# A mixed fp32 transformer stack on one core: paired splits and one bias product in the pooling mixer, side work and score banks in latent attention, the order of the NSA steps

## The chip, the cores and the metric

The kernel runs on one core of a Trainium2 chip. The metric is the device time of one execution in microseconds (us), here the median over the runs of the kernel. TensorE (PE) does the matrix products and writes PSUM, VectorE (DVE) and ScalarE (ACT) read PSUM and do the elementwise work, GpSimd (POOL) does small elementwise work in SBUF, and SyncE (SP) issues most transfers (DMAs).

## What is computed

A sequence of 512 tokens of width 1024 passes two blocks, all in fp32. Cut to what matters here:

```
first block, twice:  x = sub(x, swiglu ffn); x = sub(x, mixer); x = sub(x, swiglu ffn)
   mixer 0 = pool:   pooled[g] = centred mean over a window of 2, 4, 8, 16 tokens, group g of 256 channels
                     y = ((pooled - h)[g] @ w[g] + b[g]) * scale
   mixer 1 = mla:    lat = h @ w_in;  c_q, c_kv, k_r = split(lat), c_q and c_kv normed
                     q = c_q @ w_uq;  q_lat = q_nope @ w_uk
                     o = softmax(q_lat @ c_kv + q_rope @ k_rope) @ c_kv;  y = (o @ w_uv) @ w_o
   sub(x, f) = x + weight * (1 + gate) * norm(f(norm(x) * (1 + scale) + shift))
second block, twice: proj = norm(x) @ w_in
   y_a = stick_breaking_attention(q, k, v) * silu(z)
   y_b = (gate_c * compressed + gate_s * selected + gate_w * window attention) * silu(n_z)     (NSA)
   x = x + (sigmoid(gate_a) * (y_a @ w_up_a) + sigmoid(gate_b) * (y_b @ w_up_b)) @ w_out
```

The compressed keys and values come from blocks of 32 tokens by a small network with one hidden layer (weights `cmp_w1`, `cmp_w2`).

## The kernel before, in words

**Arithmetic.** Every fp32 operand is held as a high and a low part in a reduced format: ACT copies the high part (`split`, L244), DVE or GpSimd subtracts it from the source to get the low part (L245). A product is then three matmuls, high by high, low by high and high by low (`mm3`, L256 to L258), or two where one side is exact (`mm2`). The tiles are named `wh`, `wl` (weights), `hh`, `hl` (the normed activations), `dh`, `dl` (pooled ones), `qh`, `ql` and so on. Raw weights (`wraw`) are loaded by SP, and `split_more` (L199) splits up to three halves of 128x1024 ahead of their use.

**Order.** Each of the eight stages (ffn, pool, ffn, ffn, mla, ffn, hyb, hyb) is a list of `Item`s that `drive` (L217) runs in program order: first the weights' splits, then the item's function, then as many steps of the stage's side generator as the item's `side` gives credit for. All engines run their own instructions in the order in which this program issues them. In pool and mla the side generator (`spread`, L407) brings the three rows `rowc`, `rowb`, `rowa` of the next ffn: a DMA of each, a DMA of norm gains for two of them from ACT's queue, and a DVE product (L414) of those two.

**Pool.** The pooled difference is a banded product: per group g (0 to 3) and half z of the tokens, `band` (L702) multiplies `hh` and `hl` by constant band matrices into one bank of a two-bank PSUM tile; groups 0 and 1 share a tile, 2 and 3 another. There are four rounds over the groups: z = 0 with token tiles 0 and 1, z = 0 with tile 2, z = 1 with tiles 2 and 1, z = 1 with tile 3. At the end of the second and fourth round each group's 128x512 result is split into `dh` and `dl`. `scale` (L757) multiplies the pool weights by the output scale on DVE, `bias` (L765) splits the 1x1024 bias row, and `mix` (L772) does, per tile t and half, 12 matmuls of the pool weights and two one-row products that add the bias (L785).

**Ends of stages.** `FIN` gives, for each pair of stages, the order in which the end of one (a, b: the two product halves of a token tile; P, Z, X: norm and update of the residual `x`) is interleaved with the beginning of the next (S, A, F: norm and modulation; T: transpose; H, L: the split; G: A on GpSimd).

**Latent attention.** `lat` (L859) computes the latent of token tile t in bank `t % 2` of PSUM tile `t // 2`; `latent` norms it on DVE. `first` (L959) prepares the first four heads, then 32 units run through `attend` (L802): each iteration runs one step of several units in the order of a string. All side steps run behind `first`, whose `side` is 99.

**NSA.** In each hyb layer a preparation is written as the string `PREP`: groups of one-letter jobs, one group per item. Of its letters, a to d are the four jobs of the compression's first layer (each with two weight halves of 128x1024), w and W the window branch's projection (weights 840, 840 and 560 wide), s and q projections, p starts the norm-and-rope chain on DVE and GpSimd (reduce L1150, power L278, products L1155 to L1161), v advances it, 0 and 1 the second query projection. Capital letters A to L are fillers: gate projections of 24 matmuls of 512 columns into `gx`. `ONPOOL` names the jobs whose second half has its low part computed by GpSimd. Then 32 units (heads and branches) run through `attend` in the order of `NSO`: S scores, M row maximum, E exponential, N normalisation, T transposes, H and L their split, P the product with the values, O the fold of its result (L271), 0 and 1 further jobs: the rest of `PREP` behind the bar at 0, six matmuls of a filler at 1, from the iterations in `GAS`.

## Time and profile before

| | |
|---|---|
| median of 3 runs | 2956.75 us (2955.04 to 2959.26) |
| the profiled execution, its own time | 2962.01 us |
| its span in the trace | 2959.9 us |
| PE busy | 2806.0 us, 95% of the span |
| DVE, ACT, POOL busy | 55%, 40%, 13% |
| mean granted clock of PE | 0.962 of full speed |
| first pool products to the next ffn | about 418 to 510 us of the span |
| mla | about 1240 to 1475 us |
| NSA preparation and loop | about 2020 to 2260 us, and again 2565 to 2800 us |

A row of the timeline gives start, duration, engine, line, operation, output <- input, shape; in brackets the idle time of the engine ahead of it and what released it. PE's granted clock is 1.00 (2.4 GHz) or 0.50 (1.2 GHz); a mean between them is a mixture in time.

### The profile page before, as it was taken

The page shows a single profiled execution, that of the slowest core. Times are in us where ns is not written, and L with a number is a line of the kernel's source. Part 1 is how long each engine was busy: PE and PEld are TensorE (multiplying, and loading weights), DVE is VectorE, ACT ScalarE, POOL GpSimd, SP SyncE. Part 2 cuts the span into 40 slices and gives each one's busy share as a digit, 9 for nine tenths or more (in the row PEclk, how much of TensorE's full clock was granted, in tenths as well). Part 3 has the DMA queues.
Part 4 walks back from the last instruction along what each step waited for, and adds up shares of the span by engine and source line. Part 5 has one row for each costly group of instructions (what it writes and reads, how often), then busy time and mean ns, then how long its engine had stood idle before and what let it go on. Part 6 is the DMA issues. An engine that isn't in the chain of part 4 may idle for free.

```text
span 2959.9 us, 35318 instructions
## 1 busy us (share of the span) xinstructions
PE 2806.0 (95%) x13927; PEld 2366.0 (80%) x13927; DVE 1619.6 (55%) x2180; ACT 1169.4 (40%) x1940; POOL 376.3 (13%) x441
## 2 busy tenths in 40 slices
PE   7999988999999999979999999998899999989999
PEld 6877877888888778778788888878787887878887
DVE  5555355443355553558763233587675346767643
ACT  4223233222232223348632222384555336645531
POOL 0000012000010000147310000202131001213300
PEclk8999987999999999989999999999899999998999
DMA  7566323543336663210233333323201341231032
GB/s 242 192 202 225 107 73 107 177 169 103 107 97 198 203 204 109 60 54 30 69 117 114 100 114 95 90 62 88 63 29 58 100 142 60 76 102 37 29 100 99
DMA packets 238972, 325.74 MB, mean 110 GB/s; under 512 B 11228, under 2 KB 200896, under 8 KB 238807
## 3 DMA queue, kind: packets, MB, share of 16 engines
q1 hardware_dynamic: 237210, 317.70, 33.6%
q10 hardware_dynamic: 1596, 5.79, 0.6%
q8 instruction: 110, 1.80, 0.3%
q14 instruction: 56, 0.45, 0.0%
HBM read 317.14 MB, written 6.32 MB: 109 GB/s over the span
## 4 chain that ended last, share of the span: by engine, by line
PE 80%; DVE 8%; ACT 4%; DMA 3%; issue 2%; POOL 2%; POOLq 0%; SPq 0%; DVEq 0%; ACTq 0%
PE ps L256 21%; PE ps L257 20%; PE ps L258 20%; DMA adaw<-in_ada_w_dram 3%; PE gx L256 2%; PE gx L257 2%; PE gx L258 2%; PE pt L1248 2%; PE ps L1229 2%; DVE wl L245 1%; PE po L264 1%; PE po L263 1%; DVE wl L1027 1%; PE s L1229 1%; PE pt L1674 1%
## 5 line engine op out<-in xcount | busy, mean ns | idle before, releaser
L245 DVE TENSOR_TENSOR wl<-wraw,wh 128x1024 fp32r<-128x1024 f32 (+2 forms) x416 | 502.7, 1223 | 528.6 <-ACT wh L244 528.0
L244 ACT ACTIVATE wh<-wraw 128x1024 fp32r<-128x1024 f32 (+4 forms) x430 | 435.5, 1041 | 559.7 <-PE ps L258 308.9
L256 PE MATMUL ps<-hh,wh 128*128 128x512 f32 (+1 forms) x1648 | 639.1, 388 | 7.1 <-DVE ob L271 2.8
L257 PE MATMUL ps<-hl,wh 128*128 128x512 f32 (+1 forms) x1648 | 637.8, 387 | 2.8 <-DVE hl L468 2.8
L258 PE MATMUL ps<-hh,wl 128*128 128x512 f32 (+1 forms) x1648 | 637.2, 387 | 0.9 <-DVE wl L245 0.9
L256 PEld LDWEIGHTS ps<-hh,wh 128*128 128x128 f32 x1648 | 314.9, 191 | 71.3 <-DVE ob L271 4.2
L257 PEld LDWEIGHTS ps<-hl,wh 128*128 128x128 f32 x1648 | 314.6, 191 | 65.1 <-DVE hl L468 3.8
L258 PEld LDWEIGHTS ps<-hh,wl 128*128 128x128 f32 x1648 | 314.7, 191 | 63.2 <-DVE wl L245 1.5
L256 PE MATMUL ps<-wh,xh 128*128 128x512 f32 x800 | 313.2, 391 | 0.0
L257 PE MATMUL ps<-wl,xh 128*128 128x512 f32 x800 | 312.5, 391 | 0.0
L258 PE MATMUL ps<-wh,xl 128*128 128x512 f32 x800 | 312.3, 390 | 0.0
L361 DVE SCALAR_TENSOR_TENSOR acc<-adaw,sc,acc 128x1024 f32<-128x1024 f32 x128 | 164.1, 1282 | 151.5 <-DMA adaw<-in_ada_w_dram 151.0
L648 ACT ACTIVATE hid<-ps 128x1024 f32<-128x1024 f32 x44 | 45.1, 1028 | 400.8 <-PE ps L258 390.6
L258 PEld LDWEIGHTS ps<-wh,xl 128*128 128x128 f32 x800 | 150.6, 188 | 31.9
L256 PEld LDWEIGHTS ps<-wh,xh 128*128 128x128 f32 x800 | 150.6, 188 | 31.8
L257 PEld LDWEIGHTS ps<-wl,xh 128*128 128x128 f32 x800 | 150.6, 188 | 31.8
L277 POOL TENSOR_SCALAR s<-s 128x1 f32<-128x1 f32 x64 | 23.7, 371 | 1187.0 <-ACT junk L419 1186.1
L651 DVE TENSOR_TENSOR hid<-ps,hid 128x1024 f32<-128x1024 f32 x44 | 53.8, 1223 | 148.8 <-PE ps L258 138.9
L256 PE MATMUL gx<-hh,wh 128*128 128x512 f32 x304 | 124.3, 409 | 6.2 <-ACT scr L324 4.1
L257 PE MATMUL gx<-hl,wh 128*128 128x512 f32 x304 | 120.9, 398 | 0.0
L258 PE MATMUL gx<-hh,wl 128*128 128x512 f32 x304 | 120.9, 398 | 0.0
L256 PE MATMUL ps<-wh,hh 128*128 128x256 f32 (+3 forms) x352 | 112.8, 320 | 4.6 <-DVE scr L847 3.0
(496 smaller groups left out, 4841.5 us busy)
## 6 DMA issues: line engine op xcount, KB each, us to landing
wraw<-in_ffn_w_in_dram SPq DMA_DIRECT2D x86, 1024.0 KB
adaw<-in_ada_w_dram SPq DMA_DIRECT2D x128, 512.0 KB
wraw<-in_ffn_w_out_dram SPq DMA_DIRECT2D x88, 512.0 KB
wraw<-in_w_in_dram SPq DMA_DIRECT2D x52, 512.0 KB
wraw<-in_w_in_dram SPq DMA_DIRECT2D x14, 1024.0 KB
adaw<-in_ada_w_dram SPq DMA_DIRECT2D x32, 256.0 KB
wraw<-in_cmp_w_dram SPq DMA_DIRECT2D x16, 512.0 KB
wraw<-in_w_out_dram SPq DMA_DIRECT2D x16, 512.0 KB
```

Of the source, the lines that this page charges most:

```text
L244: self.nc.scalar.activation(h, src, AF.Copy)
L245: (eng or self.nc.vector).tensor_tensor(l, src, h.bitcast(F32), op=OP.subtract)
L256: mm(out, w[0], x[0], start=start, stop=False)
L257: mm(out, w[0], x[1], start=False, stop=False)
L258: mm(out, w[1], x[0], start=False, stop=stop)
L263: mm(out, v, xh, start=start, stop=False)
L264: mm(out, v, xl, start=False, stop=stop)
L361: nc.vector.scalar_tensor_tensor(acc, raws[q][:, k], self.sc[:, f:f + 1], acc, op0=OP.mult, op1=OP.add)
L648: nc.scalar.activation(st["hid", it], ps, AF.Silu)
L651: nc.vector.tensor_tensor(h, ps, h, op=OP.mult)
L1229: mm(sc[:, f], q[:, c], k[:, 0:n], start=m == 0 and (g == 1 or i == 0), stop=False)
L1248: nc.tensor.transpose(t[:, k], d["p"][:, f.start + k * 128:f.start + k * 128 + 128], self.ident)
```

## The change

In pool, two groups are split at once (128x1024), in the second and fourth rounds after groups 1 and 3. The bias is one tile of 128 rows, zero but for its high part in row 0 and its low part in row 32, and one product with 128 rows adds both. The scaling of weights, the bias split and the side steps stand at other items, A of tile 1 is on DVE instead of GpSimd at pool's entry, and at its exit Z of tile 1 stands behind F of tile 0. In mla the latent of tile t is in PSUM tile `t % 2`, bank `t // 2`, and the side steps run at one per four iterations. In NSA, `PREP`, `ONPOOL` and `NSO` are other strings, items with p may split four halves ahead, and one filler, L, stands in the preparation, so that five instead of six remain for the loop (iterations 6 to 25; the last number of `GAS` is not reached).

```diff
-           ("ffn", "pool"): "... b1 P1 Z1 H0 L0 a2 X1 G1 S1 b2 Z2 ..."
-           ("pool", "ffn"): "... a1 b1 Z1 P1 a2 F0 T0 X1 A1 ..."
+           ("ffn", "pool"): "... b1 P1 Z1 H0 L0 a2 X1 A1 S1 b2 Z2 ..."
+           ("pool", "ffn"): "... a1 b1 P1 a2 F0 Z1 T0 X1 A1 ..."
-    NSO, NSD, NNE = "HES1LPMNO0T", (-1, -2, -3), 1
-    PREP, ONPOOL = "s x q vv p0 ab w1 vBvWc vId vvCkJztK|uvZ e v f - - - - g - h", "csa"
+    NSO, NSD, NNE = "HE1LSMN0POT", (-1, -2, -3), 1
+    PREP, ONPOOL = "s x q vv p 0ab wL1 BvvWc vId vvCkJztK|uZ e v f - - - - g - h", "ad"
-    GAS = (6, 10, 14, 18, 22, 26)
+    GAS = (6, 10, 14, 18, 22, 28)
@@ split_more
-            if n >= self.done and (n >= self.done + 3 or ...
+            if n >= self.done and (n >= self.done + self.items[self.now].ahead or ...
@@ pool
-            st["b"] = tuple(P.tile([1, D], F32R, name=n) for n in ("pbh", "pbl"))
+            st["b"] = P.tile([128, D], F32R, name="pbhl")
+            nc.gpsimd.memset(st["b"].bitcast(F32), 0.0)
-            if last_:
+            if last_ and g % 2:
-                self.split(st["dh"][:, 2 * g:2 * g + 2, ts], st["dl"][:, 2 * g:2 * g + 2, ts], ps...)
+                self.split(st["dh"][:, 2 * g - 2:2 * g + 2, ts], st["dl"][:, 2 * g - 2:2 * g + 2, ts],
+                           st["ps", z, g // 2].rearrange("p a (m n) -> p (a m) n", m=2))
-            items.append(Item(part(g, 0, (2,), False, True, g == 0), [], g == 3))
+            items.append(Item(part(g, 0, (2,), False, True, g == 0), [], g > 1))
-            items.append(Item(part(g, 1, (2, 1), True, False, 0), [], 0))
+            items.append(Item(part(g, 1, (2, 1), True, False, 0), [], g < 2))
-            items.append(Item(part(g, 1, (3,), False, True, g == 0), [], 1 if g < 3 else 99))
+            items.append(Item(part(g, 1, (3,), False, True, g == 0), [], 0 if g < 3 else 99))
-            self.split(*st["b"], st["pb"], nc.gpsimd)
-        for k, f in ((5, lambda: scale(0)), (8, lambda: scale(1)), (15, bias)):
+            self.split(st["b"][0:1], st["b"][32:33], st["pb"])
+        for k, f in ((4, lambda: scale(0)), (12, lambda: scale(1)), (14, bias)):
-                for z in st["b"]:
-                    nc.tensor.matmul(ps[:, half], self.ones[0:1, :], z[:, half * 512:half * 512 + 512], ...)
+                nc.tensor.matmul(ps[:, half], self.ones, st["b"][:, half * 512:half * 512 + 512], ...)
@@ attend, mla
-            items.append(Item(fn, w, 0, hold))
+            items.append(Item(fn, w, side, hold))
-                o = ps[t // 2][:, t % 2, 0:416]
+                o = ps[t % 2][:, t // 2, 0:416]
-        items.append(Item(first, quad_w(0), 99))
+        items.append(Item(first, quad_w(0), 1))
-        items += self.attend(32, steps, self.ORDER, slices)
+        items += self.attend(32, steps, self.ORDER, slices, 0.25)
@@ hyb
-            items.append(Item(self.group(g, jobs), weights(g), 0, hold(g)))
+            items.append(Item(self.group(g, jobs), weights(g), 0, hold(g), 4 if "p" in g else 3))
```

VectorE in the pool stage, from the split of the second round's results to the weights' splits ahead of the products. `dl` is the low part of the pooled difference, `hl` that of the activations of token tile 3, `rowc` a row of the next ffn, `pb` the bias row. Before:

```order
L245 TENSOR_TENSOR dl<-ps,dh 128x2x256 [waits Activation_49] x2
L761 TENSOR_TENSOR wraw<-wraw,srow 128x1024 [waits DMAHW6_49,DMAHW4_49]
L245 TENSOR_TENSOR dl<-ps,dh 128x2x256 [waits Activation_49] x2
L761 TENSOR_TENSOR wraw<-wraw,srow 128x1024 [waits DMAHW5_49]
L763 TENSOR_TENSOR pb<-pb,srow 1x1024 [waits DMAHW7_49]
L468 TENSOR_TENSOR hl<-scr,hh 128x1024 [waits DVE_49,Activation_49]
L245 TENSOR_TENSOR dl<-ps,dh 128x2x256 [waits Activation_49]
L414 SCALAR_TENSOR_TENSOR rowc<-rowc,adaw 128x1024 [waits DMAHW2_49,DMAHW1_49]
L245 TENSOR_TENSOR wl<-wraw,wh 128x1024 [waits DVE_49,Activation_49]
```

With the change:

```order
L763 TENSOR_TENSOR wraw<-wraw,srow 128x1024 [waits DMAHW6_49,DMAHW4_49]
L245 TENSOR_TENSOR dl<-ps,dh 128x4x256 [waits Activation_49] x2
L414 SCALAR_TENSOR_TENSOR rowc<-rowc,adaw 128x1024 [waits DMAHW2_49,DMAHW1_49]
L468 TENSOR_TENSOR hl<-scr,hh 128x1024 [waits Activation_49]
L763 TENSOR_TENSOR wraw<-wraw,srow 128x1024 [waits DMAHW5_49]
L765 TENSOR_TENSOR pb<-pb,srow 1x1024 [waits DMAHW7_49]
L245 TENSOR_TENSOR wl<-wraw,wh 128x1024 [waits Activation_49] x2
L245 TENSOR_TENSOR dl<-ps,dh 128x4x256 [waits Activation_49]
L245 TENSOR_TENSOR pbhl<-pb,pbhl 1x1024 [waits Activation_49]
L245 TENSOR_TENSOR dl<-ps,dh 128x4x256 [waits Activation_49]
```

The splits are twice as wide and half as many, the product of `rowc` has moved ahead of `hl`, and the low part of the bias has come to this engine.

VectorE in latent attention, from the last key split (`kl`) of `first` to the second unit's row maximum (`mx`). Before:

```order
L252 TENSOR_TENSOR kl_7775<-pt,kh_7774 64x512 [waits PE_49,Activation_49]
L252 TENSOR_TENSOR kl_7777<-pt,kh_7776 64x512
L414 SCALAR_TENSOR_TENSOR rowc<-rowc,adaw 128x1024 [waits DMAHW5_49,DMAHW0_49]
L414 SCALAR_TENSOR_TENSOR rowa<-rowa,adaw 128x1024 [waits DMAHW7_49,DMAHW1_49]
L991 TENSOR_REDUCE mx<-ps 128x2 [waits PE_49] x2
L1002 RECIPROCAL mx<-mx 128x2 [waits Activation_49]
L1005 TENSOR_SCALAR p<-p,mx 128x512 [waits DVE_49]
L245 TENSOR_TENSOR ql<-pt,qh 96x512 [waits Activation_49]
L991 TENSOR_REDUCE mx<-ps 128x2 [waits PE_49]
```

With the change:

```order
L252 TENSOR_TENSOR kl_7759<-pt,kh_7758 64x512 [waits PE_49,Activation_49]
L252 TENSOR_TENSOR kl_7761<-pt,kh_7760 64x512
L991 TENSOR_REDUCE mx<-ps 128x2 [waits PE_49] x2
L1002 RECIPROCAL mx<-mx 128x2 [waits Activation_49]
L1005 TENSOR_SCALAR p<-p,mx 128x512 [waits DVE_49]
L245 TENSOR_TENSOR ql<-pt,qh 96x512 [waits Activation_49]
L414 SCALAR_TENSOR_TENSOR rowc<-rowc,adaw 128x1024 [waits DMAHW6_49,DMAHW5_49]
L991 TENSOR_REDUCE mx<-ps 128x2 [waits PE_49]
```

The products of `rowc` and `rowa` stood ahead of the first maximum; now `rowc` stands behind the first two units' steps, and `rowa` (not shown) twelve units later.

VectorE in the NSA preparation of the first hyb layer. `ob` is the last row of the norm-and-rope chain that p starts, `wl` of 1024 columns here the second half of job b, `wl` of 840 and 560 columns the window's weights. Before:

```order
L1160 TENSOR_TENSOR scr<-scr,t_0_12778 128x8x32
L1161 TENSOR_TENSOR ob<-ob,scr 128x2x256 [waits DVE_49]
L245 TENSOR_TENSOR wl<-wraw,wh 128x1024 [waits DMAHW1_49,Activation_49]
L245 TENSOR_TENSOR wl<-wraw,wh 128x840 [waits DMAHW2_49,Activation_49]
L245 TENSOR_TENSOR wl<-wraw,wh 128x840 [waits DMAHW7_49,DMAHW3_49,Activation_49]
L245 TENSOR_TENSOR wl<-wraw,wh 128x560 [waits DMAHW4_49,Activation_49]
```

With the change, the chain's beginning (`nv` is a split of the s job's result, `r` the chain's reductions):

```order
L252 TENSOR_TENSOR nv_14024<-gx,nv_14024 128x2x64 [waits Activation_49]
L252 TENSOR_TENSOR nv_14024<-gx,nv_14024 128x2x64
L245 TENSOR_TENSOR wl<-wraw,wh 128x1024 [waits DMAHW0_49,Activation_49]
L245 TENSOR_TENSOR wl<-wraw,wh 128x1024 [waits DMAHW1_49,Activation_49]
L1150 TENSOR_REDUCE r_14086<-scr 128x8
```

and its end:

```order
L1160 TENSOR_TENSOR scr<-scr,t_0_12762 128x8x32
L1161 TENSOR_TENSOR ob<-ob,scr 128x2x256 [waits DVE_49]
L245 TENSOR_TENSOR wl<-wraw,wh 128x840 [waits DMAHW2_49,Activation_49]
L245 TENSOR_TENSOR wl<-wraw,wh 128x840 [waits DMAHW7_49,DMAHW3_49,Activation_49]
L245 TENSOR_TENSOR wl<-wraw,wh 128x560 [waits DMAHW7_49,Activation_49]
L245 TENSOR_TENSOR wl<-wraw,wh 128x1024 [waits DMAHW0_49,Activation_49]
```

Both halves of job b now stand ahead of the chain; the window's splits still stand behind its last row, and the split of the moved filler L (1024 columns) behind them.

## Rows read from the trace of the kernel before

**Rows 1.** The page, part 1: busy time of the engines, share of the span, instructions.

```profile
PE 2806.0 (95%) x13927; PEld 2366.0 (80%) x13927; DVE 1619.6 (55%) x2180; ACT 1169.4 (40%) x1940; POOL 376.3 (13%) x441
```

**Rows 2.** Windows: start:end, length, busy time (x instructions) of PE, PEld, DVE, ACT, POOL, PE's granted clock, DMA share, GB/s.

```profile
426.00:453.50 27.50, 19.34 (x88) 18.53 (x87) 15.70 (x18) 9.50 (x13) 2.84 (x3) 0.50 0.39 127
457.00:474.00 17.00, 17.00 (x64) 13.51 (x63) 11.48 (x10) 4.99 (x8) 2.40 (x6) 0.51 0.01 1
...
1305.00:1450.00 145.00, 136.12 (x882) 121.24 (x882) 127.92 (x217) 123.87 (x280) 104.63 (x101) 0.98 0.07 22
2187.67:2202.13 14.46, 14.46 (x96) 12.84 (x94) 10.26 (x30) 8.34 (x27) 5.65 (x5) 1.00 0.15 51
```

**Rows 3.** Timeline of PE in the pool stage: the rounds, the first products, the end.

```profile
419.94 0.33 PE L721 MATMUL ps<-wh,hl 128*128 128x136 f32 x1 [1.38 <-DVE hl L468]
...
429.98 0.38 PE L716 MATMUL ps<-wh,hh 128*128 128x8 f32 x1 [1.80 <-DVE dl L245]
...
435.01 0.56 PE L716 MATMUL ps<-wh,hh 128*128 128x256 f32 x1
...
441.84 0.46 PE L716 MATMUL ps<-wh,hh 128*128 128x136 f32 x1
...
449.38 0.48 PE L716 MATMUL ps<-wh,hh 128*128 128x136 f32 x1 [1.77 <-DVE dl L245]
...
450.73 0.52 PE L256 MATMUL ps<-wh,dh 128*128 128x256 f32 x1
...
454.98 0.49 PE L785 MATMUL ps<-pbl,ones 1*128 1x512 f32 x1 [1.02 <-POOL pbl L245]
...
457.22 0.79 PE L785 MATMUL ps<-pbh,ones 1*128 1x512 f32 x1
...
458.37 0.58 PE L256 MATMUL ps<-wh,dh 128*128 128x256 f32 x1
...
486.25 1.06 PE L451 MATMUL ps<-ident,scr 128*128 128x128 f32 x8 [2.45 <-DVE scr L442]
```

**Rows 4.** Timeline of POOL and of DVE in the pool stage.

```profile
412.39 2.41 POOL L438 TENSOR_TENSOR scr<-x,rowa 128x1024 f32<-128x1024 f32 x1 [2.94 <-DVE x L529]
...
438.70 1.21 DVE L468 TENSOR_TENSOR hl<-scr,hh 128x1024 fp32r<-128x1024 f32 x1
```

**Rows 5.** Timeline of PE in latent attention: second latent, first scores of the loop.

```profile
1271.51 0.43 PE L256 MATMUL ps<-wh,hh 128*128 128x416 f32 x1 [2.48 <-DVE scr L847]
...
1305.03 0.80 PE L256 MATMUL ps<-kh,qh 96*128 96x512 f32 x1 [6.09 <-ACT p L997]
```

**Rows 6.** Timeline of DVE in latent attention, around the loop's start.

```profile
1296.92 1.39 DVE L252 TENSOR_TENSOR kl<-pt,kh 64x512 fp32r<-64x512 f32 x2 [0.46 <-ACT kh L250]
1299.75 1.22 DVE L414 SCALAR_TENSOR_TENSOR rowc<-rowc,adaw 128x1024 f32<-128x1024 f32 x1 [1.44 <-DMA adaw<-in_norm_g_dram]
...
1302.27 2.36 DVE L991 TENSOR_REDUCE mx<-ps 128x2 f32<-128x1024 f32 x2
```

**Rows 7.** Timeline of PE, then of DVE, in the first NSA preparation.

```profile
2050.94 0.48 PE L257 MATMUL pt<-wl,qAh 128*64 128x256 f32 x1 [8.45 <-DVE wl L245]
...
2053.58 0.43 PE L257 MATMUL ps<-wl,hh 128*128 128x280 f32 x1
...
2038.48 1.91 DVE L1150 TENSOR_REDUCE r<-scr 128x8 f32<-128x512 f32 x4
...
2049.66 3.10 DVE L245 TENSOR_TENSOR wl<-wraw,wh 128x1024 fp32r<-128x1024 f32 x3
```

**Rows 8.** Timeline of PE in the first NSA loop: scores of two units, a filler.

```profile
2138.39 0.46 PE L1229 MATMUL s<-kth,qAl 128*128 128x128 f32 x1
...
2144.52 0.31 PE L1229 MATMUL s<-kth,qAl 128*128 128x128 f32 x1
...
2152.26 0.40 PE L256 MATMUL gx<-hh,wh 128*128 128x512 f32 x1
2152.49 0.39 PE L257 MATMUL gx<-hl,wh 128*128 128x512 f32 x1
```

More of the change, by code (lines that the diff above doesn't have):

```diff
@@ L101, with __init__ @@
 class Item:
-    def __init__(self, fn, w=(), side=1, hold=0):
-        self.fn, self.w, self.side, self.hold = fn, list(w), side, hold
+    def __init__(self, fn, w=(), side=1, hold=0, ahead=3):
+        self.fn, self.w, self.side, self.hold, self.ahead = fn, list(w), side, hold, ahead
 class Kern:
     FIN = {("ffn", "ffn"): "a0 b0 P0 Z0 X0 S0 A0 a1 F0 b1 P1 Z1 a2 T0 X1 H0 A1 b2 S1 L0 F1 P2 Z2 a3 T1 X2 H1 L1 w0 G2 b3 P3 S2 Z3 X3 A3 F2 S3 F3||T2 H2 T3 H3 L2 L3",
[2 rows of a table removed]
[2 rows of a table added]
            ("ffn", "mla"): "a0 b0 P0 Z0 X0 S0 A0 F0 a1 b1 a2 P1 T0 Z1 X1 A1 H0 S1 L0 b2 F1 P2 Z2 w0 X2 a3 T1 H1 S2 A2 b3 Z3 F2 P3 L1 X3 G3 T2|H2 S3 L2 F3 T3|H3 L3",
@@ L201, in split_more @@
             n = self.nsplit
-            if n >= self.done and (n >= self.done + 3 or self.halves[n].item - self.now > self.halves[n].late or (n >= SLOTS and self.halves[n - SLOTS].last > self.now - back)):
+            if n >= self.done and (n >= self.done + self.items[self.now].ahead or self.halves[n].item - self.now > self.halves[n].late or (n >= SLOTS and self.halves[n - SLOTS].last > self.now - back)):
                 break
@@ L783, in product @@
                                  g % 2 == 0 and k == 0, False)
-                for z in st["b"]:
-                    nc.tensor.matmul(ps[:, half], self.ones[0:1, :], z[:, half * 512:half * 512 + 512], start=False,
-                                     stop=z is st["b"][1])
+                nc.tensor.matmul(ps[:, half], self.ones, st["b"][:, half * 512:half * 512 + 512], start=False, stop=True)
                 return ps.rearrange("p a b -> p (a b)") if half else None
@@ L800, in parts, with attend @@
         return lanes, w, hold
-    def attend(self, n, steps, order, slices):
+    def attend(self, n, steps, order, slices, side=0):
         items = []
```

1 line of the change is left out of this document (removed), and 4 rows, old and new, of the table FIN.

## The prediction

> **What bounds the kernel now.** The page first: PE is busy 2806.0 of 2959.9 us, 95% [rows 1]. Nearly all of the program is PE's own work, so the change can win only where PE waits or runs at half clock. I therefore read PE's timeline for waits of the three stages that the diff touches, then the engine that released each wait, then windows for the clock.
>
> In **pool**, PE is busy 19.34 of 27.50 us between 426 and 453.5, at a granted clock of 0.50, that is 1.2 GHz [rows 2]. Four of its waits there are for a `dl` split of DVE: 1.80 is the first, 1.77 the last, the two between are 2.29 and 1.41, 7.3 us in all [rows 3]. They are false ones. The waiting matmul writes the second bank of a PSUM tile whose first bank is being split for the group before; nothing that it needs is missing. In the products PE is busy all the time from 457 to 474 and still has 0.51 of its clock [rows 2].
>
> In **latent attention** PE waits 2.48 us for the norm of the tile before, which sits in the other bank of its PSUM tile, and 6.09 us before the loop [rows 5]. DVE's rows show why the second is so long: the last key split ends at 1298.31, `rowc` then waits 1.44 for its gains, two products follow, and only at 1302.27 comes the maximum on which the first exponential rests [rows 6].
>
> In **NSA** the largest wait of each preparation is 8.45 us, for the low part of the second half of job b [rows 7]; the second hyb layer has the same wait. DVE does that split at 2049.66, behind the norm-and-rope chain that began at 2038.48.
>
> **Pool, part by part.** Splitting in pairs takes the four waits away: the round's next group starts in the bank beside, nobody reads that tile. Gain 7.3 us. The order shows no PE wait on DVE there any more except those for `hl` and the bands' low parts. A of tile 1 moves from GpSimd, 2.41 us [rows 4], to DVE, where the wide rows take 1.21 [rows 4]; PE's wait of 1.38 on `hl` at 419.94 [rows 3] is behind it, so 1.2. The first product then starts at 450.73 - 8.5 = 442.2 [rows 3].
>
> What could be late instead is `hl` of token tile 3, for the fourth round. It was done at 438.70 + 1.21 = 439.9 [rows 4], two us ahead of that round at 441.84 [rows 3]; now the round begins 1.2 + 1.80 + 2.29 = 5.3 us sooner, at 436.5, and on DVE two wide splits and `rowc`'s product stand ahead of `hl`. From the end of the second round, which lies one round of 441.84 - 435.01 = 6.8 us earlier [rows 3], it takes a wide copy on ACT, a wide subtraction, `rowc` and `hl`, about 1.1 + 1.2 + 1.2 + 1.2 = 4.7. That leaves two us. `rowc`'s product also waits for a DMA of gains; in latent attention that wait was 1.44 [rows 6]. So I cost it at nothing; beyond two us, each us of the DMA is one of PE.
>
> The bias: eight pairs of one-row products become eight products. A pair paces 458.37 - 457.22 = 1.15 us at half clock [rows 3]; a 512-column matmul takes 0.23 at full clock [rows 8], so about 0.46 at half. That is 0.7 each, 5.5 in all at half clock, half of that at full. The wait of 1.02 on GpSimd's low part [rows 3] goes too: DVE does it. Not all of this arrives, because the stage ends on a chain of norms and updates, shown by PE's 2.45 us wait for DVE at 486.25 [rows 3]. Bounds: nothing and 6.5; I take 4.4, since PE is busy without a pause through most of the products. Z of tile 1 behind F of tile 0 is DVE work moved within that chain; I put it into the bounds. Sum for pool: 7.3 + 1.2 + 4.4 = 12.9.
>
> **The clock in the products.** The row shows PE busy for all 17.00 us and the clock at 0.51 [rows 2]: being busy did not bring the clock back for most of them. The Trainium skill says otherwise ("TensorE: Matmul & The Clock Gate", Part 1, "What's actually happening"): the half rate is the idle state, and sustained matmul activity releases it. By that page these products, with PE never idle, should run at 2.4 GHz, and 17.00 us of work would take 8.5 less. The sum above goes by the row, with no change in clock; the other outcome is a rival below.
>
> **Latent attention.** With tile t in PSUM tile `t % 2`, the second latent writes where nothing is read: 2.48 gone. The third now waits for the norm of the first, done long before. Taking the two `rowc`/`rowa` products from ahead of the maximum lets DVE begin at 1298.3 instead of 1302.27: 4.0. They cost 1.22 each inside the loop [rows 6], where DVE is busy 127.92 and PE 136.12 of 145 us [rows 2]. Neither engine is full, so of the 2.4 I charge half. Sum: 2.5 + 4.0 - 1.2 = 5.3. Bounds: 0.1 if the loop's start is held by something else and both products cost in full; 6.5 if they cost nothing there.
>
> **NSA, each of two layers.** Both splits of b now stand ahead of the chain, so the 8.45 us wait for b goes. But the window's splits still stand behind the chain, and PE wants the window next. The chain starts one split of 1.1 us later, and a split of 1024 columns takes 3.10 / 3 = 1.0, so one of 840 about 0.9 [rows 7]: window data at about 2049.66 + 1.1 + 0.9 = 2051.7, against 2053.3 when PE began it before (its second matmul is at 2053.58 [rows 7]). So the wait is not removed but moved by one job, and 1.6 is what is gained; it would be 8.45 if the window came in time, and nothing if the added splits push the chain more.
>
> The filler L, 24 matmuls of 0.23 us [rows 8], is 5.45 us of PE work that moves from loop iterations 26 to 29 into the preparation; there it stands behind a late split and fills no wait. Without it four units of the loop can be faster than now. Now four units take 14.46 us with PE busy for all of it [rows 2], 3.61 each. The units before the fillers begin took (2144.52 - 2138.39) / 2 = 3.06 [rows 8], so 2.2 is gained for four; DVE's 10.26 us for four [rows 2] bounds the gain at 4.2. I take 3.2. The new order inside the loop (S behind the filler, O behind P) I cost at nothing, since PE has no wait there to begin with; what covers it is the slack of the other engines, and what it costs without that is the last rival. Sum per layer: 1.6 - 5.45 + 3.2 = -0.7, two layers -1.4, with bounds of +7.2 and -5.5 for each.
>
> **Sum.** 12.9 + 5.3 - 1.4 = 16.8 us. The profiled execution took 2962.01, 5.3 above the median of the runs, 2956.75; so 2945.2 for it, and 2940 as a median.
>
> **The rivals.**
>
> The clock comes back in the products. For it: the one-row products, which use one of 128 rows, and the waits ahead of the products are gone. Against: the windows' 0.51 at a full PE. Time: 2940 - 8.5 = 2931.5. Chance 0.18.
>
> The NSA wait really goes, because the window's splits come in time. For it: halves may now be split four ahead; against: the order still has them behind the chain. It would give 2 x (8.45 - 1.6) = 13.7 more: 2926. Chance 0.08.
>
> The last units of the loop do not become faster, since each waits for its own exponentials and folds, and L is paid in full: 2 x 3.2 = 6.4 less gain, 2946. Chance 0.16.
>
> The change does not free the rounds in pool: `hl` of tile 3 is late by the DMA of the gains, and the 8.5 us come back as one wait. 2948.5. Chance 0.06.
>
> Slower: S now stands behind the filler instead of ahead of it, so that in a unit with a filler the next scores, their maximum and their exponential come 6 x 0.23 = 1.4 us later [rows 8]. Where that chain through DVE and ACT has less slack than this, PE's transposes wait for it in each of the 2 x 20 units with fillers. Half of the 1.4 showing makes 40 x 0.7 = 28: 2968. The gain of the rest is used up from 0.42 a unit on. For it: the chain goes through three engines, and DVE is busy for 10.26 of the 14.46 us of four units [rows 2]. Against: PE shows no wait at all there now, and S is issued a whole unit before its transposes. Chance 0.06.
>
> **How the numbers follow.** The forecast keeps 0.46, with a range of its own of 2933 to 2947 from the bounds of bias, `rowc` and loop. The range of 8 in 10, 2923 to 2951, takes in all rivals but the slower one. A measurement of this kernel can tell 0.2%, about 6 us, from no change. Faster by more: 0.85. Within: 0.09, for cases where the third and fourth rivals meet. Slower: 0.06.
>
> **What would show it.** Right: no PE wait on `dl` between 426 and 450, the first product about 8.5 us earlier; the wait before the loop of latent attention at about 2 us; in NSA no wait for b, but one of 6 to 8 us for a window split; loop units of 3.61 us with fillers and about 2.8 without. Wrong: a wait on `hl` in the fourth round, units above 3.7 us with fillers, or a preparation longer by over 5 us.

## The result and the profile after

The changed kernel takes 2926.25 us (median of 3 runs, 2925.72 to 2930.96) against 2956.75: a ratio of 0.99 with a 95% interval of 0.9886 to 0.9913. That is 30.5 us less, where 16.8 were forecast. The time lies in the range, but below the likeliest case's own 2933 to 2947. Timed again beside the last two experiments, the same kernel took 2927.5 against 2957.54 (0.9903, 0.9888 to 0.9917).

The profiled execution took 2930.96, with a span of 2929.2, against 2962.01 and 2959.9. The page's first part, to be held against [rows 1]: PE is busy for 17.6 us less, and 13.1 of the 30.7 are time in which it stood.

```profile
PE 2788.4 (95%) x13919; PEld 2352.2 (80%) x13919; DVE 1619.1 (55%) x2180; ACT 1168.4 (40%) x1936; POOL 365.1 (12%) x438
```

Where they went is read from the stages. I cut the span at PE instructions that both kernels have: pool from its first band product to the wait of the next ffn for its weights; latent attention from its first latent to its first scores, and from there to the output projection; each NSA layer from the transposes behind the stick-breaking branch to the first window product, to the first compressed scores, and to the merge. Windows of the kernel before (columns as in [rows 2]): pool, latents, attention loop, then preparation and loop of the first NSA layer and of the second.

```profile
417.60:503.30 85.70, 66.21 (x353) 58.30 (x352) 51.03 (x50) 31.76 (x47) 22.08 (x26) 0.72 0.28 93
1247.90:1295.50 47.60, 36.19 (x162) 32.66 (x160) 20.63 (x47) 14.84 (x38) 20.22 (x37) 0.82 0.18 60
1295.50:1451.70 156.20, 139.80 (x900) 123.73 (x898) 136.40 (x226) 129.30 (x290) 104.63 (x101) 0.98 0.09 29
2053.30:2122.10 68.80, 61.90 (x367) 54.08 (x365) 41.86 (x80) 34.15 (x66) 11.92 (x14) 0.94 0.39 105
2122.10:2257.20 135.10, 126.09 (x749) 111.83 (x750) 100.94 (x264) 78.16 (x223) 45.72 (x34) 0.88 0.09 28
2597.60:2665.20 67.60, 61.15 (x366) 53.68 (x364) 41.96 (x80) 34.26 (x66) 11.94 (x14) 0.95 0.40 107
2665.20:2798.10 132.90, 123.48 (x750) 109.65 (x750) 100.93 (x264) 78.65 (x223) 45.72 (x34) 0.90 0.10 29
```

The same stages of the changed kernel:

```profile
417.60:489.80 72.20, 54.54 (x346) 51.99 (x345) 50.99 (x48) 30.95 (x42) 21.85 (x26) 0.81 0.33 110
1233.80:1275.10 41.30, 32.85 (x161) 30.17 (x160) 20.61 (x47) 14.86 (x38) 20.02 (x37) 0.88 0.15 44
1275.10:1428.10 153.00, 138.86 (x899) 122.91 (x897) 136.90 (x226) 129.71 (x290) 108.13 (x101) 0.99 0.11 36
2020.90:2100.10 79.20, 68.21 (x388) 59.77 (x388) 51.42 (x95) 35.76 (x69) 14.95 (x18) 0.91 0.35 95
2100.10:2226.70 126.60, 115.83 (x726) 101.62 (x726) 98.47 (x263) 76.43 (x221) 43.38 (x33) 0.93 0.09 26
2558.30:2638.90 80.60, 69.38 (x389) 60.45 (x389) 51.40 (x95) 36.34 (x69) 14.90 (x18) 0.89 0.35 94
2638.90:2767.40 128.50, 119.08 (x725) 105.04 (x725) 99.12 (x263) 76.02 (x221) 43.24 (x33) 0.89 0.08 26
```

Pool is 13.5 us shorter, the latents 6.3, the attention loop 3.2. The piece ahead of the window, not in these rows, falls from 34.7 to 26.3 us in both NSA layers, since its wait of 8.45 is gone and 1.20 is left; with it the preparation is 2.0 and 4.6 longer and the loop 8.5 and 4.4 shorter. So the first layer gains 6.5, and the second loses 0.3. 13.5 + 6.3 + 3.2 + 6.5 - 0.3 = 29.2 of the 30.7 in the span; the rest lies in stages that the change doesn't touch.

**Pool.** PE's timeline of the changed kernel shows no wait for `dl` any more. Ahead of the fourth round its other waits were there before too: 0.78 for the second tile's `hl` (1.38 [rows 3]), 2.09 for the bands' low parts (2.08), 1.04 for the third tile's `hl` (0.88). In the fourth round there is a new one, of 2.12, for the last tile's `hl`; the first product comes 26.6 us after the first band product instead of 33.1 [rows 3]. The bias is one product of 128 rows.

```profile
419.33 0.33 PE L722 MATMUL ps<-wh,hl 128*128 128x136 f32 x1 [0.78 <-DVE hl L468]
...
439.50 0.48 PE L722 MATMUL ps<-wh,hl 128*128 128x136 f32 x1 [2.12 <-DVE hl L468]
...
444.26 0.52 PE L256 MATMUL ps<-wh,dh 128*128 128x256 f32 x1
...
449.90 0.41 PE L786 MATMUL ps<-pbhl,ones 128*128 128x512 f32 x1
450.15 0.28 PE L256 MATMUL ps<-wh,dh 128*128 128x256 f32 x1
...
451.59 0.40 PE L786 MATMUL ps<-pbhl,ones 128*128 128x512 f32 x1
```

DVE's timeline says what that 2.12 is: after the second round's two wide splits DVE stands at `rowc`'s product for 4.64 us, for the DMA of the gains, and `hl` is behind it in the queue.

```profile
431.22 1.23 DVE L245 TENSOR_TENSOR dl<-ps,dh 128x1024 fp32r<-128x1024 f32 x1 [0.23 <-ACT dh L244]
437.08 1.23 DVE L414 SCALAR_TENSOR_TENSOR rowc<-rowc,adaw 128x1024 f32<-128x1024 f32 x1 [4.64 <-DMA adaw<-in_norm_g_dram]
438.23 1.22 DVE L468 TENSOR_TENSOR hl<-scr,hh 128x1024 fp32r<-128x1024 f32 x1
```

**Latent attention.** The 2.48 us ahead of the second latent [rows 5] are gone, and the wait at the loop's start is 2.19 instead of 6.09. DVE goes from the last key split straight to the maximum; `rowc` comes inside the loop.

```profile
1280.70 0.50 PE L256 MATMUL ps<-kh,qh 96*128 96x512 f32 x1 [2.19 <-ACT p L997]
```

```profile
1276.52 1.39 DVE L252 TENSOR_TENSOR kl<-pt,kh 64x512 fp32r<-64x512 f32 x2 [0.47 <-ACT kh L250]
1277.95 2.36 DVE L991 TENSOR_REDUCE mx<-ps 128x2 f32<-128x1024 f32 x2
```

**NSA.** The wait for b of 8.45 [rows 7] is gone; one of 6.22 for the window's low part stands in its place, and 1.20 ahead of it. L begins at 2036.45 (first NSA layer, PE).

```profile
2020.89 0.37 PE L256 MATMUL ps<-wh,hh 128*128 128x280 f32 x1 [1.20 <-DVE scr L1155]
2027.48 0.60 PE L257 MATMUL ps<-wl,hh 128*128 128x280 f32 x1 [6.22 <-DVE wl L245]
...
2036.45 0.39 PE L256 MATMUL gx<-hh,wh 128*128 128x512 f32 x1
```

In the loop, units with a filler keep their pace (2156.24 to 2199.52, 12 units, 3.61 us each, as in [rows 2]). The four that lost theirs are this window: 9.74 us, 2.44 each.

```profile
2199.52:2209.26 9.74, 9.24 (x70) 8.27 (x68) 8.36 (x27) 6.74 (x23) 4.31 (x3) 1.00 0.00 1
```

### The profile page after: what moved, and what is told of

Read it like the earlier page. It is cut to its first block, busy times and chain, and to the rows that moved or that the text cites. A ratio compares the mean times of both kernels' runs of the same rounds, so it can differ in the third digit from the quotient of the medians.

```text
span 2929.2 us, 35287 instructions
## 1 busy us (share of the span) xinstructions
PE 2788.4 (95%) x13919; PEld 2352.2 (80%) x13919; DVE 1619.1 (55%) x2180; ACT 1168.4 (40%) x1936; POOL 365.1 (12%) x438
## 4 chain that ended last, share of the span: by engine, by line
PE 78%; DVE 9%; DMA 4%; ACT 4%; issue 3%; POOL 2%; SPq 0%; DVEq 0%; POOLq 0%; ACTq 0%
PE ps L257 20%; PE ps L256 20%; PE ps L258 20%; DMA adaw<-in_ada_w_dram 3%; PE gx L256 2%; PE gx L257 2%; PE gx L258 2%; PE ps L1229 2%; PE pt L1248 2%; DVE wl L245 1%; PE po L264 1%; PE po L263 1%; DVE wl L1027 1%; DVE mx L991 1%; PE pt L1674 1%
## 5 line engine op out<-in xcount | busy, mean ns | idle before, releaser
L245 DVE TENSOR_TENSOR wl<-wraw,wh 128x1024 fp32r<-128x1024 f32 (+1 forms) x418 | 504.9, 1223 | 525.8 <-ACT wh L244 525.1
L244 ACT ACTIVATE wh<-wraw 128x1024 fp32r<-128x1024 f32 (+3 forms) x430 | 436.0, 1041 | 572.5 <-PE ps L258 308.1
L277 POOL TENSOR_SCALAR s<-s 128x1 f32<-128x1 f32 x64 | 26.3, 410 | 1200.4 <-ACT junk L419 1199.3
L256 PE MATMUL gx<-hh,wh 128*128 128x512 f32 x304 | 126.6, 417 | 6.5 <-ACT scr L324 4.1
L257 PE MATMUL ps<-wl,hh 128*128 128x256 f32 (+3 forms) x352 | 112.5, 320 | 12.4 <-DVE wl L245 12.4
```

What stands on the lines that cost most here:

```text
L244: self.nc.scalar.activation(h, src, AF.Copy)
L245: (eng or self.nc.vector).tensor_tensor(l, src, h.bitcast(F32), op=OP.subtract)
L256: mm(out, w[0], x[0], start=start, stop=False)
L257: mm(out, w[0], x[1], start=False, stop=False)
```

## Experiments

Stage lengths in us as defined above, each from one profiled execution; "prep" is both pieces of an NSA preparation together.

| kernel | median (runs) | pool, to first product / rest | latents / loop | NSA 1, prep / loop | NSA 2, prep / loop |
|---|---|---|---|---|---|
| before | 2956.75 (3) | 33.1 / 52.6 | 47.6 / 156.2 | 103.5 / 135.1 | 102.3 / 132.8 |
| changed | 2926.25 (3) | 26.6 / 45.5 | 41.3 / 153.1 | 105.5 / 126.6 | 106.9 / 128.5 |
| pool alone | 2940.24 (4) | 26.8 / 46.8 | 46.4 / 155.7 | 103.3 / 135.0 | 102.3 / 132.9 |
| pairs alone | 2947.68 (1) | 25.0 / 53.0 | 43.8 / 156.5 | 103.3 / 135.1 | 102.3 / 132.9 |
| bias alone | 2953.02 (1) | 33.1 / 49.2 | 46.6 / 155.7 | 104.7 / 133.2 | 102.4 / 132.9 |
| latent attention alone | 2948.88 (9) | 33.1 / 49.7 | 40.1 / 152.8 | 103.4 / 135.1 | 102.3 / 132.9 |
| side steps alone | 2958.16 (1) | 33.1 / 52.5 | 44.7 / 154.4 | 103.6 / 135.1 | 102.4 / 132.9 |
| NSA alone | 2946.12 (5) | 33.1 / 52.5 | 44.4 / 156.0 | 105.6 / 128.3 | 106.3 / 128.4 |
| changed, old loop order | 2928.34 (1) | 27.7 / 45.3 | 41.3 / 153.5 | 105.9 / 126.4 | 106.9 / 127.6 |
| changed, L in the loop | 2944.86 (1) | 26.3 / 45.4 | 40.1 / 152.4 | 105.7 / 133.2 | 107.3 / 133.2 |
| changed, old prep with L | 2924.40 (1) | 26.9 / 45.3 | 39.9 / 153.0 | 107.0 / 127.4 | 109.6 / 127.4 |
| changed, `hl` first | 2928.08 (4) | 24.3 / 45.4 | 40.1 / 152.3 | 105.8 / 127.3 | 106.8 / 128.5 |

Kernels that were timed together share their runs of the kernel before: 2955.95 for the four with several runs here, 2954.07 and 2954.13 for those with one. A single time says little (the last 7 runs of the kernel before spread from 2950.39 to 2959.9); of those kernels the stages are read.

**The three parts alone.** First pool's lines of the diff in the kernel before, then those of latent attention, then those of NSA; the cores of them are:

```diff
-            if last_:
+            if last_ and g % 2:
...
+                nc.tensor.matmul(ps[:, half], self.ones, st["b"][:, half * 512:half * 512 + 512], start=False, stop=True)
```

> The kernel before with the pool part of the change alone (paired splits, one bias product, the items of scaling, bias and side steps, both FIN strings); latent attention and NSA are the old code. Theory 1 (the sum by stages): the pool stage, from its first band product to the next ffn's wait for its weights, is 13.5 us shorter, as in the changed kernel, so about 2943 us. Of the two NSA stages, whose code is untouched, theory 1a says that their length depends on where the granted clock happens to fall in them, so that one of them (238.6 and 235.1 us before, from the last transposes of the stick-breaking part to the merge's first product) differs by over 2 us from before; theory 1b says that a stage with the same code keeps its length within 1 us, and that what the changed kernel won in the first NSA stage (6.5 us) and not in the second (0.3 us lost) comes from its own edit.

```diff
-                o = ps[t // 2][:, t % 2, 0:416]
+                o = ps[t % 2][:, t // 2, 0:416]
...
-        items.append(Item(first, quad_w(0), 99))
+        items.append(Item(first, quad_w(0), 1))
```

> The kernel before with the latent attention part alone (PSUM banks of the latent, side steps spread over the loop). Theory 1: 9.4 us shorter in that stage, as in the changed kernel, so about 2947 us: 2.5 from the latent's wait, 4 from the loop's start, 3 from the half clock that no longer follows the 6 us wait. Rival: the loop pays for the two row products, the stage gains the forecast 5.3 and the rest of the changed kernel's gain there comes from the pool part's shift in time; then about 2951. The untouched NSA stages test the clock as in the run of the pool part: over 2 us different in one of them by theory 1a, within 1 us by 1b.

```diff
-    PREP, ONPOOL = "s x q vv p0 ab w1 vBvWc vId vvCkJztK|uvZ e v f - - - - g - h", "csa"
+    PREP, ONPOOL = "s x q vv p 0ab wL1 BvvWc vId vvCkJztK|uZ e v f - - - - g - h", "ad"
```

> The kernel before with the NSA part alone (PREP, ONPOOL, NSO, four halves ahead). Theory 1a (the edit gives back in the preparation what it wins in the loop, and the clock decides the rest): between 2953 and 2960, and the two NSA stages change by different amounts. Rival 1b (the edit itself is worth about 6 us in the first layer): the first stage is 6.5 us shorter again and the second 0.3 us longer, about 2950.5. In both the wait of 8.45 us for job b is gone and one of about 6.2 us for the window's low part stands in its place.

Measured: 0.9947 (0.993 to 0.9964), 0.9978 (0.9967 to 0.9988) and 0.9965 (0.9952 to 0.9978) of the kernel before, which is 15.7, 7.1 and 9.8 us less. Together 32.6; the whole change had 30.5. The parts add up within their uncertainty. By the medians each of them gains more than its term of the forecast; the intervals, about 11 to 21, 4 to 10 and 7 to 14 us, leave that open for pool (12.9 forecast) and latent attention (5.3), and not for NSA (-1.4). By its stages the NSA part alone gains 5.0.

The second NSA layer, where a kernel leaves it alone, keeps its length however far the program ahead of it has moved: it is within 102.3 to 102.4 and 132.8 to 132.9 in all six kernels with the old NSA lines. Other stages don't. The stretch ahead of the pool stage took 409.3 to 417.6 us in the 14 profiled executions, though the edits reach no more than its last items; in the stretch from 20 to 40 us the granted clock was 0.66 in the kernel before and 0.80 in the changed kernel with the old preparation and L, which are the two ends. So a single time can differ by 8 us without the edit. The latents vary too: with the old lines between 43.8 and 47.6, with the new ones between 39.9 and 41.3. So some of the 6.3 us of the profiled pair is scatter, and the kernel with latent attention alone, timed in nine runs, gives the better size, 7.1 (3.5 to 9.8) for that whole part.

**Pairs alone and bias alone.** Pool's gain, taken apart.

```diff
-            if last_:
+            if last_ and g % 2:
```

> The kernel before with the paired splits of pool alone: the two one-row bias products, the items of scaling and side steps and both FIN strings stay old. Theory (two separate gains): the four waits for dl go, the first product comes about 7 us after fewer than before (33.1 us after the first band product before, about 26 here), and the rest of the stage keeps its 52.6 us with some 11 us lost to the half clock, since the one-row products are still there. Rival (the waits are what keeps the clock low): the rest shrinks as well, by 5 us or more, with less half clock in it, as in the run of the whole pool part (46.8).

```diff
-                for z in st["b"]:
-                    nc.tensor.matmul(ps[:, half], self.ones[0:1, :], z[:, half * 512:half * 512 + 512], start=False,
-                                     stop=z is st["b"][1])
+                nc.tensor.matmul(ps[:, half], self.ones, st["b"][:, half * 512:half * 512 + 512], start=False, stop=True)
```

> The kernel before with the one bias product of 128 rows (and its low part on VectorE) alone. Theory: the first product stays at 33.1 us, the rest of the pool stage shrinks from 52.6 to about 47, because the clock is back at its full level for most of the products: eight one-row pairs, during which one of 128 rows works, are gone. Rival: the clock stays, and only the shorter products count: the rest shrinks by 2 to 4 us.

Each part does its own half of the stage: the pairs bring the first product 8.1 us sooner (33.1 to 25.0) and leave the rest at 53.0; the bias leaves the first and shortens the rest by 3.4. What the bias does besides its own instructions shows in windows of 17 us in the products, to be held against 457 to 474 of the kernel before, with PE busy all the time at 0.51 [rows 2]. With the pairs of splits alone, one-row products kept:

```profile
446.00:463.00 17.00, 17.00 (x64) 13.50 (x63) 11.08 (x10) 4.59 (x8) 2.85 (x6) 0.50 0.03 13
```

With the 128-row product alone:

```profile
451.50:468.50 17.00, 11.41 (x76) 10.70 (x75) 14.45 (x13) 5.72 (x12) 3.92 (x10) 0.80 0.01 2
```

And in the changed kernel:

```profile
450.50:467.50 17.00, 12.05 (x95) 11.01 (x93) 14.55 (x12) 8.38 (x13) 6.67 (x11) 1.00 0.01 1
```

The stretch with a 128-row product runs at 2.4 GHz, that with one-row products mostly at 1.2. It is not a clean switch. Of the 96 products of 256 columns, counted in PE's timeline, those that took 0.40 us or less (0.41 and more is half clock) were 40 to 42 in four of the kernels with one-row products (before, pairs, NSA, side steps alone), 63 in the fifth (latent attention alone), and 71 to 78 in the nine executions with the 128-row product. In the kernel with 63 the clock came up between one-row products; it fell again 1.2 us behind a wait of 1.68 and then stayed low with PE busy:

```profile
446.00:463.00 17.00, 14.46 (x82) 11.69 (x83) 9.02 (x8) 5.86 (x9) 5.34 (x7) 0.89 0.37 132
463.00:470.00 7.00, 7.00 (x30) 5.90 (x29) 6.69 (x6) 3.29 (x5) 1.48 (x4) 0.53 0.01 2
```

```profile
462.19 1.06 PE L451 MATMUL ps<-ident,scr 128*128 128x128 f32 x8 [1.68 <-DVE scr L442]
```

In the changed kernel PE waits 2.51 and 1.72 us at the same step, and the products behind those waits stay at full clock. Two things differ between the two kinds of bias product, the rows (1 or 128) and the number (two or one), and no run takes them apart.

With bias alone the last bias product comes 24.4 us after the first product instead of 29.4, with PE busy for 18.6 of them instead of 28.4, and yet the stage's rest is only 3.4 shorter: among the products PE now waits for DVE's step of the norm.

```profile
460.94 1.94 PE L451 MATMUL ps<-ident,scr 128*128 128x128 f32 x8 [5.46 <-DVE scr L442]
```

DVE is late there because the product of `rowa` has stood 4.01 us for the DMA of its row, with the norm's steps behind it in the queue:

```profile
452.31 1.23 DVE L414 SCALAR_TENSOR_TENSOR rowa<-rowa,adaw 128x1024 f32<-128x1024 f32 x1 [4.01 <-DMA rowa<-vec]
```

In the changed kernel, whose side steps stand at other items, that product comes at 447.53 without a wait, and the first wait of PE of that kind is 2.51. With the whole pool part the rest is 45.3 to 46.8, shorter than with the bias alone. The side steps, the scaling of the weights and the two FIN strings were not run by themselves, so what each of them has of this is not shown.

**`hl` first.** The changed kernel with `rowc`'s product behind `hl`, by the side credits of the second and fourth rounds.

```diff
-            items.append(Item(part(g, 0, (2,), False, True, g == 0), [], g > 1))
+            items.append(Item(part(g, 0, (2,), False, True, g == 0), [], g == 2))
...
-            items.append(Item(part(g, 1, (2, 1), True, False, 0), [], g < 2))
+            items.append(Item(part(g, 1, (2, 1), True, False, 0), [], 0))
...
-            items.append(Item(part(g, 1, (3,), False, True, g == 0), [], 0 if g < 3 else 99))
+            items.append(Item(part(g, 1, (3,), False, True, g == 0), [], (3, 0, 0, 99)[g]))
```

> The changed kernel with the product of rowc on VectorE moved behind hl of token tile 3 (side steps at other items of pool). In the changed kernel that product waits 4.64 us for the DMA of the gains, hl stands behind it, and PE waits 2.12 us for hl in the fourth round. Theory: that wait goes, the first product of pool comes 2.1 us sooner, about 2924 us. Rival: the products wait for the weights' low parts instead, which now stand behind the late rowc; then the first product moves by less than 1 us and the time stays at 2926. A shift of the clock's spells may add or take some us to either in later stages.

`hl` is now done before the fourth round wants it, the gains are waited for behind it, and the first product comes 24.3 us after the first band product, 2.3 sooner:

```profile
431.83 1.22 DVE L468 TENSOR_TENSOR hl<-scr,hh 128x1024 fp32r<-128x1024 f32 x1
...
436.43 1.23 DVE L414 SCALAR_TENSOR_TENSOR rowc<-rowc,adaw 128x1024 f32<-128x1024 f32 x1 [1.13 <-DMA adaw<-in_norm_g_dram]
```

So the wait of 2.12 was the gains' DMA, one wait in the place of others. The median of 2928.08 (0.9903, 0.9888 to 0.9919) is not below that of the changed kernel, so both were timed once more, in turn, in five rounds.

> The changed kernel itself once more, beside the next one, so that the two are timed in turn on one chip: 2924 to 2931 as it was.

> The changed kernel with the gains' product behind hl in pooling, once more. Its pool stage was 2.5 us shorter (the wait of 2.12 for hl is gone) in one profiled execution each, while the medians did not differ. Theory: the 2.5 us are real and last, so this one is 1.5 to 3 below the other of the same call. Rival: the chain that ends the pool stage, or what half clock the stages behind it have, takes them back: within 1 us of each other.

Pool took 71.4 and 69.7 us, the medians were 2927.5 (2926.93 to 2930.0) and 2924.15 (2918.75 to 2927.71), the ratios 0.9903 (0.9888 to 0.9917) and 0.9884 (0.9865 to 0.9902). The stage is shorter by about two us each time; for the kernel the intervals overlap, and the two pairs of medians disagree in sign. It beats the kernel before; that it beats the changed one is not shown.

**Side steps alone.** The two credits of latent attention, with the latents' banks as before.

```diff
-        items.append(Item(first, quad_w(0), 99))
+        items.append(Item(first, quad_w(0), 1))
...
-        items += self.attend(32, steps, self.ORDER, slices)
+        items += self.attend(32, steps, self.ORDER, slices, 0.25)
```

> The kernel before with the two side credits of latent attention alone (the first loop item 99 to 1, the loop's items 0 to 0.25); the banks of the latent products stay as they were. Theory: the loop's wait for the side work goes (6.09 us at its start falls to about 2), the latent stretch falls by 3 to 4 to some 44 us, and the loop falls from 156.2 to about 153 because no stretch of it runs at half clock; the 2.48 us wait between the latent products stays. Layer 197 to 198, kernel 2949 to 2952. Rival of the forecast's own sum: the loop has two more row products and gets 1.2 us longer, layer near 201, kernel 2953 to 2954.

The 6.09 us at the loop's start became 2.22, and the 2.49 between the latents stayed:

```profile
1267.33 0.43 PE L256 MATMUL ps<-wh,hh 128*128 128x416 f32 x1 [2.49 <-DVE scr L847]
...
1297.07 0.50 PE L256 MATMUL ps<-kh,qh 96*128 96x512 f32 x1 [2.22 <-ACT p L997]
```

The loop is 1.8 us shorter where 3.9 of wait went, at the same granted clock of 0.98, so 2.1 of other waits came in; I put them down to the two products. With the banks as well (latent attention alone) it is 3.4 shorter. That the kernel's single time is not lower is within the spread of single times.

**The loop's order.** The changed kernel with the old string of steps.

```diff
-    NSO, NSD, NNE = "HE1LSMN0POT", (-1, -2, -3), 1
+    NSO, NSD, NNE = "HES1LPMNO0T", (-1, -2, -3), 1
```

> The changed kernel with the old order string of the NSA loop (S ahead of the filler, the fold behind M and N). Theory: the loop's gain over before (8.5 us in the first layer, 4.3 in the second) comes from the missing filler (2 to 4 us of each) and from less half clock, and the order string is worth under 1.5 us per layer: loops of 126 to 128 us and 128 to 130. Rival: the order string is what lets the loop start and end sooner; then the loops are 3 us or more longer than 126.6 and 128.5.

Loops of 126.4 and 127.6 against 126.6 and 128.5 (and 128.2 and 128.6 in the second execution of the changed kernel). The order of the steps is worth nothing that can be told here; the forecast's slower rival, S behind the filler, has no price.

**L back in the loop.** The changed kernel, with the sixth filler in iterations 26 to 29 again.

```diff
-    PREP, ONPOOL = "s x q vv p 0ab wL1 BvvWc vId vvCkJztK|uZ e v f - - - - g - h", "ad"
+    PREP, ONPOOL = "s x q vv p 0ab w1 BvvWc vId vvCkJztK|uZ e v f - - - - g - h", "ad"
...
-    GAS = (6, 10, 14, 18, 22, 28)
+    GAS = (6, 10, 14, 18, 22, 26)
```

> The changed kernel with the filler L back in the loop (iterations 26 to 29), all else as changed. Theory: the preparation, from the window's first product to the first compressed scores, is 5.5 us or more shorter than the changed kernel's 79.2 and 80.6 us, the loop 2 to 4 us longer per layer, so that leaving L in the loop is better by 1 to 3 us per layer: about 2922. Rival: L in the preparation keeps the clock up there, and the loop without it ends sooner by as much as L costs: no difference, or the changed kernel ahead by 2 us or more per layer.

Without L the preparation is not shorter: 105.7 and 107.3 against 105.5 and 106.9. In L's place PE waits 3.34 us for the norm-and-rope products of DVE, a wait that the changed kernel does not have:

```profile
2028.18 0.60 PE L257 MATMUL ps<-wl,hh 128*128 128x280 f32 x1 [6.22 <-DVE wl L245]
...
2050.56 0.37 PE L256 MATMUL ps<-wh,hh 128*128 128x280 f32 x1 [3.34 <-DVE scr L1155]
```

In the loop L costs 6.6 and 4.7 us. So L's move is worth 6.8 and 5.1, and the other edits of the preparation, without L, lose 2.2 and 5.0 in the preparation (105.7 and 107.3 against 103.5 and 102.3).

What makes up these differences can be read from the second piece of the preparation (2021.59 to 2101.01 and 2566.23 to 2647.23 in this kernel). In the first layer PE stands there for 14.6 us without L and for 11.0 with it; the other part of L's price comes back by the clock, 0.89 without it and 0.91 with it. What the other edits lose is mostly clock as well. Against the kernel before, over both pieces, PE stands for 15.8 us instead of 15.4 in the first layer and 15.8 instead of 14.9 in the second, but it is busy 1.9 and 4.2 us longer with the same number of products. The granted clock in the second piece is 0.89 and 0.85, where it was 0.94 and 0.95.

**The old preparation with L.** The changed kernel, with the steps and the splits of the preparation as before, but L behind w.

```diff
-    PREP, ONPOOL = "s x q vv p 0ab wL1 BvvWc vId vvCkJztK|uZ e v f - - - - g - h", "ad"
+    PREP, ONPOOL = "s x q vv p0 ab wL1 vBvWc vId vvCkJztK|uvZ e v f - - - - g - h", "csa"
...
-            items.append(Item(self.group(g, jobs), weights(g), 0, hold(g), 4 if "p" in g else 3))
+            items.append(Item(self.group(g, jobs), weights(g), 0, hold(g), 3))
```

> The changed kernel, but the NSA preparation keeps the order of before (steps, splits on the vector engine or not, three items ahead) with the one step L put in behind w; so the loop has lost L as in the change. Theory: what the NSA part gains comes from L's absence in the loop alone, and the other edits of the preparation only pull a wait for b out of it and put a wait for wl in. Then the first NSA layer keeps its loop near 127 us and its stretch up to the window goes back from 26.3 to 34.7, with a preparation of 69 to 72, some 231 to 234 in all; the second layer 34.7 + 69 + 128, some 231 to 233; kernel 2922 to 2929. Rival: only in the new order is there a gap that L fills, and in the old order L costs its full 5 us on PE in the preparation: then the preparation is 74 or more, the layers 236 to 238, the kernel 2930 to 2934.

The wait for b is there again with its 8.44 us, and L is not free: the preparation is 3.5 and 7.3 longer than before. The layers take 234.4 and 237.0, against 232.1 and 235.4 in the changed kernel's first profiled execution and 234.1 and 234.9 in its second. Neither theory was right alone: the NSA part's gain is L's absence from the loop, L costs 3.5 and 7.3 in the old order and nothing in the new one, which has a gap for it but loses 2.2 and 5.0 itself. What the two orders with L differ by is 0.3 to 2.3 us a layer. The kernel's one time of 2924.4, below the changed kernel's median, says nothing against this: the stretch ahead of its pool stage is the shortest of all, 409.3 us.

```profile
2014.80 0.47 PE L257 MATMUL pt<-wl,qAh 128*64 128x256 f32 x1 [8.44 <-DVE wl L245]
```

## Why the prediction was right, and where it was off

- **Pool, the waits.** Right in mechanism: the four `dl` waits were false, and the pairs alone bring the first product 8.1 us sooner. Of the whole change 6.5 arrive, not 8.5. The step "I cost it at nothing", for `rowc`'s product ahead of `hl`, failed: two us of slack were seen, the gains' DMA held DVE for 4.64, and 2.12 came back as a wait. A of tile 1 on DVE was priced at 1.2 and gave 0.6, the wait of 1.38 that became 0.78. The late `hl` was the fourth rival, in part: the bound "beyond two us, each us of the DMA is one of PE" had the right form.
- **Pool, the bias.** 4.4 were forecast; the stage's rest is 7.1 shorter in the whole change, and 3.4 with the bias alone, where a late product of `rowa` on DVE takes back part of it. The bound of 6.5 counted only the replaced instructions. The rival of the returning clock was right in kind, not in its 8.5: the products run at a granted clock of 1.00 in the changed kernel, and bias alone shows that the bias product brings it and the pairs don't. It was put second with 0.18 because PE was full at 0.51 before; that the one-row products were the difference was named as its reason and weighed too little. The Trainium skill ("TensorE: Matmul & The Clock Gate", Part 1, "What's actually happening") says that sustained matmul activity releases the half rate. With 128-row products the trace agrees; with one-row products between them it does not, with PE busy for 17.00 of 17.00 us at 0.50.
- **Latent attention.** 5.3 forecast, 9.5 in the profiled pair, 7.1 by the medians of that part alone. Both waits went as said, the second to 2.19 as "about 2". The loop's term was right in size (3.2 for 4.0 - 1.2 = 2.8); the latents' was not, 6.3 for 2.5. Their granted clock is 0.88 instead of 0.82, which the sum did not have, and part of it is the scatter of that stage. The charge of half of 2.4 for the moved products was, with the side steps alone, 2.1.
- **NSA, the wait.** Right: not removed but moved by one job, 6.22 in the forecast's 6 to 8. From the layer's first transposes to the second window product it is 32.88 us instead of 34.94 (2027.48 - 1994.60; 2053.58 [rows 7] - 2018.64), a gain of 2.06 for the 1.6 said. It does not last: the preparation loses it again behind that point, to the clock (the run with L in the loop).
- **NSA, L.** This step failed: "it stands behind a late split and fills no wait". It fills the 3.34 us that PE would next wait for DVE's norm-and-rope products, and taking it out makes the preparation no shorter. The 5.45 were charged for nothing.
- **NSA, the loop.** "I take 3.2", with 4.2 as the bound by DVE, was too low. The 3.06 us a unit behind it came from rows at half clock for the most part: the granted clock from 2138.39 to 2144.52 is 0.63 in the kernel before. The four units fell to 2.44 us each, which is 4.7 less; the second layer's loop lost 4.4, the first 8.5. DVE's 10.26 for four units [rows 2] was no bound: in the window without the filler it is busy 8.36. PE had no wait in those units, so all of L's 5.45 could come off, and that row should have set the price.
- **Between the layers.** Why the first gains 6.5 and the second nothing was not forecast. The rows give the place: the first loop's granted clock rises from 0.88 to 0.93, the second's falls from 0.90 to 0.89, and the second preparation's falls from 0.95 to 0.89. In the second execution of the changed kernel the layers gain 4.5 and 0.2, so the difference is in part scatter. Why the same instructions get another clock in the second layer was not tried and stays open.

Taken together: the direction was right, and for pool and latent attention by the mechanisms given, with the clock left out of the sums. NSA was forecast as a loss of 1.4 and is a gain of 4 to 6 us by the stages of five executions. Of the 13.9 us by which the profiled pair exceeds the sum, NSA has 7.6, latent attention 4.2 and pool 0.6; 1.5 lie in stages that the change doesn't touch. Pool's 13.5 for 12.9 is partly luck, since the waits gave 2 less and the rest of the stage 2.7 more. That the median lies at 2926, the time of the second rival, is luck too: the wait of that rival did not go.

## What to carry to other kernels

Find the wait that a filler can cover before you price the filler: ask not which wait stands at its place now but which comes next when the work ahead of it is gone. In the loop here, where PE was full, removed PE work counted almost in full, 4.7 of 5.45 us; DVE's busy time shrank with it and was no floor. Check the granted clock of a row before you take a price from it. A bias as one product of 128 rows instead of two of one row took more off PE's busy time than its own instructions (9.8 us among the products with the bias alone, where eight pairs of 1.15 replaced by 0.43 at half clock make 5.8), so look at the granted clock of a busy stretch and at what stands between its large products; and look which DMA the next engine waits for once PE is faster.

## What the runs showed of the hardware

- A stretch with PE busy all the time can stay at 1.2 GHz. With two one-row products of 512 columns behind every 12 of 256 columns and 128 rows, PE was busy 17.00 of 17.00 us at 0.50; with one 128-row product instead, the granted clock was 0.80 and 1.00 in windows of the same place. With the one-row products it could also come up, and then it fell again 1.2 us behind a wait of 1.68 us (latent attention alone, 463 to 470: busy 7.00 of 7.00, 0.53); with the 128-row product waits of 2.51 and 1.72 us had no such fall behind them (changed kernel).
- At full clock the pair of one-row products still paced 0.64 us (latent attention alone, 455.25 to 455.89), the single product 0.23 to 0.25 (changed kernel, 449.90 to 450.15).
- A stage's length repeats within 0.2 us in kernels that leave it alone where its clock repeats (the second NSA layer in six kernels), and scatters where it doesn't: by 4 us in the latents (43.8 to 47.6), by 8 in the stretch ahead of the pool stage (409.3 to 417.6).
